# The state-space layer's small products sent to the two halves of the array in turn

## The chip, the cores and the metric

The kernel runs on one core of one Trainium2 chip. A time is the device time of one execution, in microseconds (us). Three timed runs of the kernel before took 2817.99, 2818.27 and 2820.51 us; the median is 2818.27.

## The reference, cut to what matters

One hybrid decoder block on 528 tokens (16 learned ones and 512 of the sequence) of width 2048, all in float32: attention and a state-space layer run side by side on the same normalised input, are mixed by gates, projected, and followed by a dense feed-forward layer. The part that the change touches is the state-space layer, 64 groups of 16 channels, each with 64 complex states:

```python
def s5_scan(u, lam_re, lam_im, log_step, b_re, b_im, c_re, c_im, d):
    ...
    bu_re = jnp.einsum('blgp,gnp->blgn', uf, bb_re)
    bu_im = jnp.einsum('blgp,gnp->blgn', uf, bb_im)
    ...
    _, _, x_re, x_im = lax.associative_scan(combine, (a_re, a_im, bu_re, bu_im), axis=1)
    y = (jnp.einsum('blgn,gpn->blgp', x_re, c_re.astype(f32))
         - jnp.einsum('blgn,gpn->blgp', x_im, c_im.astype(f32))
         + d.astype(f32) * uf)
    return y
```

## The kernel before, in words

The weights stream from HBM in blocks of 128 x 1024. ScalarE rounds each block to a high part `whi` (L261), VectorE subtracts to get the low part `wlo` (L262), and every product of the dense layers is three matmuls (high by high, high by low, low by high). `Weights.use()` splits two blocks ahead of the one in use; three buffers hold raw blocks, three the split ones. TensorE works through the dense layers block by block (`dense()`, L369: eight k-tiles of three matmuls of 512 columns per block).

The state-space layer is a background program: the generator `ssm()` (L508). After each dense block `bg()` (L354) lets it emit work until it has yielded more than the 3.6 us of credit that the block gives; the numbers behind `yield` are prices written by hand. So its instructions stand between dense blocks in TensorE's one queue, in an order that is fixed when the program is built.

The time axis is cut into 66 chunks of 8 steps, and the 64 groups into four batches of 16 (8 pairs `j` with two members `g2` each). In a batch TensorE does four things:

- Kernel taps, `pk` (L667 to L670): for each pair the taps of lags 0 to 7, 128 rows (lag and channel) by 32 columns. The weights `BL` are 128 columns wide; the real and the imaginary part are two products that add up. 16 products. VectorE adds the direct term, and eight DMAs write the taps to HBM (`kd`), from where eight other DMAs build the triangular `TT`.
- Transposes of `BL` (L679), eight of 128 x 128, which ScalarE copies out of PSUM (L680).
- Chunk sums, `pS` (L710 to L717): 32 products of 64 weight columns and 66 moving columns in two bursts. The two members `g2` of a pair write partitions 0 to 63 and 64 to 127 in turn, and each product is a sum by itself.
- Outputs, `pys` (L748 to L753): 64 products of 64 weight columns and 64 moving columns. Each output half `r` of each group is the sum of two, one of `TT` with the inputs `U` and one of `C2` with the states `X2`. `pys[0]` is the PSUM tile V, `pys[1]` the tile Q. All products of the first half (partitions 0 to 63) come first, then, behind a `yield`, all of the second.

In the trace the helper `mm` is L315, so these products are told apart by their tiles: `psQ<-sC,ssA` is `pk`, `psD<-U,ssB` is `pS`, `<-U,ssB` into psV or psQ is the `TT` product (`TT` lies in the buffer ssB) and `<-w,ER` the `C2` product (`X2` lies in w, `C2` in ER). The trace has two records, a weight load (LDWEIGHTS) and a matmul each, for one of these float32 products: the 16 products of `pk` are 32 records.

The code names in full:

Of the kernel before, what the change touches and what calls it, by code (L numbers as in the profile page):

```python
# [30 lines left out]
P = 128  # L31
# [17 lines left out]
BP = 8  # L49
# [236 lines left out]
def build(tc, A, out):  # L286
    nc = tc.nc
    ctx = ExitStack()
    with ctx:
        sp = ctx.enter_context(tc.tile_pool(name="sp", bufs=1))  # L290
        pp = ctx.enter_context(tc.tile_pool(name="pp", bufs=1, space=bass.MemoryType.PSUM))
        dp = ctx.enter_context(tc.tile_pool(name="dp", bufs=1, space=bass.MemoryType.DRAM))
        ctx.enter_context(tc.manual_schedule())
        _emit(nc, sp, pp, dp, A, out)


def _emit(nc, sp, pp, dp, A, out):
# [3 lines left out]
    def sb(shape, dt, tag, bufs=1):  # L301
        cnt[0] += 1
        return sp.tile(shape, dt, tag=tag, name=f"{tag}_{cnt[0]}", bufs=bufs)
# [3 lines left out]
    def ps(shape, tag):  # L307
        cnt[0] += 1
        return pp.tile(shape, F32, tag=tag, name=f"ps{tag}_{cnt[0]}", bufs=BANKS[tag])
# [4 lines left out]
    def mm(o, l, r, start, stop, more=False):  # L314
        PE.matmul(o, lhsT=l, rhs=r, start=start, stop=stop, skip_group_check=more)  # L315
# [5 lines left out]
    def tt(o, a, b, op, eng=DVE):  # L321
        eng.tensor_tensor(o, a, b, op=op)  # L322
# [148 lines left out]
    def halves(tag0, tag1):  # L471
        return [(ps([P, 512], tag0)[:, :HT], 0, HT), (ps([P, 512], tag1)[:, :HT], HT, T)]

    pend = []
    for j in range(8):
        if j == 2:
            d2 = ps([P, 2, 512], "D")
            o = [(d2[:, 0, :HT], 0, HT), (d2[:, 1, :HT], HT, T)]
        else:
            o = halves("A", "B")  # L480
# [24 lines left out]

    MAGIC = 12582912.0

    def ssm():  # L508
        prm = sb([P, 3, 32], F32, "sprm")
        POOL.dma_start(prm, A["sprm"])  # L510
# [99 lines left out]
        for b in range(4):  # L610
# [6 lines left out]
            Ct = sb([P, 2, BP, 48], F32, "sC")  # L617
# [26 lines left out]
            BL = sb([P, 2, BP, CL * 16], F32, "ssA")  # L644
# [20 lines left out]

            pk = ps([P, 512], "Q")
            for j in range(BP):  # L667
                o = pk[:, j * 32:(j + 1) * 32]
                mm(o, BL[:, 0, j], Ct[:, 0, j, 16:48], True, False)
                mm(o, BL[:, 1, j], Ct[:, 1, j, 16:48], False, True)  # L670
            tt(Dg, pk[:, :BG * 16], Dg, ADD)
            for i in range(CL):
                POOL.dma_start(kd[:, g0:g0 + BG, i], Dg[i * 16:(i + 1) * 16].rearrange("p (g o) -> p g o", o=16))
# [36 lines left out]
            for h in range(2):  # L710
                pS = ps([P, 2, 512], "D")
                for jl in range(4):
                    j = h * 4 + jl
# [31 lines left out]
            yield 3.4  # L745
            Y = sb([P, BG, 64], F32, "T1")
            pys = [ps([P, BP, 64], "V"), ps([P, BP, 64], "Q")]
            for r in (slice(0, 64), slice(64, P)):  # L748
                for j in range(BP):
                    for g2 in range(2):  # L750
                        mm(pys[g2][r, j], TT[:, 2 * j + g2, r], U[:, 2 * j + g2, 2:66], True, False)
                        mm(pys[g2][r, j], C2[:, g2, j, r], X2[:, g2, j, 1:65], False, True)
                yield 0.1  # L753
            for g2 in range(2):
                ACT.activation(Y[:, g2::2], pys[g2], AF.Copy)
            yield 3.4
# [5 lines left out]

    left = {"kr", "kv", "q"}
    bg_gen[0] = ssm()
    kvl = sb([P, 4, T], F32, "ssA")
    acc_kv = sb([P, T], F32, "acc")
    for j in range(4):
        o = halves("A", "B")
# [8 lines left out]
    o = halves("A", "B")  # L777
# [801 lines left out]
    def down(fs, ot, c, w):  # L1579
        p = ps([P, 512], "AB"[ot % 2])  # L1580
        o = p[:, :c.stop - c.start]
        for n_, f in enumerate(fs):
            wh, wl = w(ot * len(fs) + n_)
            x = acts[f][:, :, c]
            mm(o, wh, x[:, 0], n_ == 0, False)
            mm(o, wh, x[:, 1], False, False)
            mm(o, wl, x[:, 0], False, n_ == len(fs) - 1)
        return o
# [30 lines left out]
    for h, c in ((0, lo_), (1, hi_)):  # L1619
        for ot in range(KT):  # L1620
            o = down(LAST, ot, c, resident)
# [31 lines left out]
```

## Time and profile before

| | |
|---|---|
| median of the three runs | 2818.27 us |
| the profiled execution | 2820.02 us |
| its span, first to last instruction | 2818.2 us |
| TensorE matmuls busy | 2776.5 us, 99% of the span |
| TensorE weight loads busy | 2562.7 us, 91% |
| VectorE / ScalarE / GpSimd busy | 1908.8 / 1135.9 / 413.8 us |
| mean granted TensorE clock | 0.996 of full |

How to read the rows below. A row of a timeline begins with its start and its length in us, then engine, line, operation, output<-inputs, shapes and a count: "x32" are 32 records that follow each other, and the length runs from the first start to the last end. A number in square brackets is the idle time of that engine ahead of the row and what ended it. PE is the matmul side of TensorE, PEld its weight loads. Matmul records overlap (the next starts while the last is still draining), so what a product costs is read from start to start, not from the length of a record. A row of the view by stretches has the stretch, its length, the busy time and the count of records on each engine, then the granted clock, the share of DMA time and GB/s.

### The profile page before, as it was taken

What the parts mean: (1) busy time and instruction counts of PE and PEld (TensorE: products, weight loads), DVE (VectorE), ACT (ScalarE), POOL (GpSimd) and SP (SyncE); (2) the same over time, 40 slices, a digit from 0 to 9 for tenths busy, and PEclk for the clock granted to TensorE, in tenths of its full rate; (3) what the DMA queues carried; (4) which work ended last, traced back from release to release, by engine and by line L of the source; (5) the groups of instructions that cost most, each with busy time, mean ns of one, the idle gap of its engine ahead of it and who ended that gap; (6) DMA issues with size and microseconds to landing.
All of it is one profiled execution on the core that took longest, in us unless ns stands there. A gap on an engine that the chain in (4) does not pass through costs nothing.

```text
span 2818.2 us, 47282 instructions
## 1 busy us (share of the span) xinstructions
PE 2776.5 (99%) x19526; PEld 2562.7 (91%) x19526; DVE 1908.8 (68%) x2609; ACT 1135.9 (40%) x1625; POOL 413.8 (15%) x633
## 2 busy tenths in 40 slices
PE   9999999999999999999999999999999999999997
PEld 8988888889999788888889999999999998999997
DVE  6467456556666433343468888888888888788896
ACT  5123222225555432222234444444444445353445
POOL 2012221222111000111212000000000003030112
PEclk9999999999999999999999999999999999999999
DMA  5333443542222243334433343333333337474542
GB/s 192 106 117 115 128 142 112 139 132 88 63 68 72 94 142 110 122 116 139 134 128 137 133 150 127 128 135 135 137 129 139 128 128 258 161 261 173 199 161 98
DMA packets 114631, 378.86 MB, mean 134 GB/s; under 512 B 16720, under 2 KB 21584, under 8 KB 114352
## 3 DMA queue, kind: packets, MB, share of 16 engines
q1 hardware_dynamic: 76672, 263.36, 27.5%
q0 software_dynamic: 36320, 109.29, 12.3%
q10 hardware_dynamic: 1424, 3.21, 0.5%
q8 instruction: 153, 2.51, 0.4%
q14 instruction: 62, 0.51, 0.1%
HBM read 316.04 MB, written 51.97 MB: 131 GB/s over the span
## 4 chain that ended last, share of the span: by engine, by line
PE 92%; DVE 3%; DMA 2%; issue 1%; ACT 1%; POOL 0%; DVEq 0%; ACTq 0%; POOLq 0%
PE psA L315 60%; PE psB L315 19%; PE psQ L315 6%; PE psV L315 5%; PE psD L315 2%; DVE S L322 1%; DVE wlo L262 1%; DMA S<-td 0%; DVE ev L322 0%; ACT whi L261 0%; DMA ER<-td 0%; PE psA L1024 0%; DMA T<-td 0%; DMA ssB<-td 0%; DMA raw<-in_wst 0%
## 5 line engine op out<-in xcount | busy, mean ns | idle before, releaser
L315 PE MATMUL psA<-S,whi 128*128 128x256 f32 (+2 forms) x5440 | 1306.6, 327 | 16.9 <-ACT whi L261 6.3
L315 PEld LDWEIGHTS psA<-S,whi 128*128 128x128 f32 x5440 | 921.4, 188 | 115.7 <-ACT whi L261 7.7
L315 PE MATMUL psA<-S,wlo 128*128 128x256 f32 (+2 forms) x2720 | 889.8, 327 | 0.0
L262 DVE TENSOR_TENSOR wlo<-raw,whi 128x1024 fp32r<-128x1024 f32 (+1 forms) x479 | 592.3, 1238 | 310.3 <-ACT whi L261 308.1
L261 ACT ACTIVATE whi<-raw 128x1024 fp32r<-128x1024 f32 (+1 forms) x479 | 504.1, 1054 | 534.7 <-PE psA L315 254.6
L315 PEld LDWEIGHTS psA<-S,wlo 128*128 128x128 f32 x2720 | 513.2, 189 | 47.3
L315 PE MATMUL psB<-S,whi 128*128 128x256 f32 (+1 forms) x1392 | 285.0, 283 | 0.1
L262 DVE TENSOR_TENSOR wlo<-cmb,whi 128x1024 fp32r<-128x1024 f32 x180 | 219.9, 1221 | 67.6 <-ACT whi L261 66.6
L261 ACT ACTIVATE whi<-cmb 128x1024 fp32r<-128x1024 f32 x180 | 190.4, 1058 | 171.3 <-DVE wlo L262 125.0
L315 PEld LDWEIGHTS psB<-S,whi 128*128 128x128 f32 x1392 | 227.1, 189 | 0.3 <-PE psD L315 0.3
L315 PE MATMUL psB<-S,wlo 128*128 128x256 f32 (+1 forms) x696 | 195.9, 281 | 1.5 <-DVE wlo L262 1.5
L315 PEld LDWEIGHTS psB<-S,wlo 128*128 128x128 f32 x696 | 131.6, 189 | 1.7 <-DVE wlo L262 1.7
L1312 POOL DMA_DIRECT2D td<-sC x22 | 15.8, 718 | 754.9 <-ACT ev L1384 712.0
L322 DVE TENSOR_TENSOR H<-psA,ev 128x512 f32<-128x512 f32 x32 | 22.1, 690 | 85.2 <-PE psA L315 85.2
L836 ACT ACTIVATE ev<-ev 128x512 f32<-128x512 f32 x32 | 20.2, 632 | 146.8 <-DVE ev L322 146.8
L242 DVE TENSOR_TENSOR cmb<-raw,raw 128x1024 f32<-128x1024 f32 x60 | 73.1, 1219 | 8.8 <-DMA raw<-in_wst 8.7
L322 POOL TENSOR_TENSOR acc<-acc,ev 128x512 f32<-128x512 f32 (+2 forms) x43 | 53.4, 1241 | 162.0 <-ACT ev L1615 80.6
L315 PE MATMUL psA<-H,whi 128*128 128x264 f32 (+2 forms) x312 | 76.5, 334 | 0.6 <-DVE ev L322 0.5
L242 DVE TENSOR_TENSOR cmb<-cmb,raw 128x1024 f32<-128x1024 f32 x60 | 73.2, 1220 | 0.0
L242 DVE TENSOR_TENSOR raw<-raw,raw 128x1024 f32<-128x1024 f32 x60 | 73.1, 1218 | 0.0
L242 DVE TENSOR_TENSOR cmb<-raw,cmb 128x1024 f32<-128x1024 f32 x60 | 73.1, 1218 | 0.0
L315 PE MATMUL psB<-ssA,whi 128*128 128x256 f32 (+1 forms) x340 | 72.5, 303 | 0.0
(630 smaller groups left out, 4982.9 us busy)
## 6 DMA issues: line engine op xcount, KB each, us to landing
raw<-in_wst SPq DMA_DIRECT2D x485, 512.0 KB, 3.6
td<-sC POOLq DMA_DIRECT2D x22, 512.0 KB, 3.2
td<-H POOLq DMA_DIRECT2D x40, 256.0 KB, 3.3
S<-td POOLq DMA_DIRECT2D x40, 256.0 KB, 8.0
sg<-ev POOLq DMA_DIRECT2D x32, 256.0 KB, 2.3
ev<-sg POOLq DMA_DIRECT2D x32, 256.0 KB, 3.0
U<-ER POOLq DMA_DIRECT2D x64, 64.0 KB, 2.0
ev<-in_xT POOLq DMA_DIRECT2D x16, 256.0 KB, 3.0
```

The source lines that it names most:

```text
L242: self.nc.vector.tensor_tensor(t, g(a), g(b), op=op)
L261: self.nc.scalar.activation(hi[:, a:b], w[:, a:b], AF.Copy)
L262: self.nc.vector.tensor_tensor(lo[:, a:b], w[:, a:b], hi[:, a:b], op=ALU.subtract)
L315: PE.matmul(o, lhsT=l, rhs=r, start=start, stop=stop, skip_group_check=more)
L322: eng.tensor_tensor(o, a, b, op=op)
L836: ACT.activation(e, e, AF.Sigmoid)
L1312: POOL.dma_start(td[pr, 0:2].rearrange("f p n -> p f n"), Cu)
```

## The change

`pk` is cut into output halves: each of its 16 products of 128 weight columns becomes two of 64, one per half of the PSUM partitions, so 32 products. The products of `pys` stay 64, but the loop over the halves moves inward: each `TT` product of the first half is followed by that of the second, then the two `C2` products. The two chunks of `pys` are now cut by pairs (four and four) and not by halves; there are as many yields at the same prices.

```diff
+    RH = slice(0, 64), slice(64, P)
...
             for j in range(BP):
-                o = pk[:, j * 32:(j + 1) * 32]
-                mm(o, BL[:, 0, j], Ct[:, 0, j, 16:48], True, False)
-                mm(o, BL[:, 1, j], Ct[:, 1, j, 16:48], False, True)
+                for i in range(2):
+                    for r in RH:
+                        mm(pk[r, j * 32:(j + 1) * 32], BL[:, i, j, r], Ct[:, i, j, 16:48], i == 0, i == 1)
...
-            for r in (slice(0, 64), slice(64, P)):
-                for j in range(BP):
-                    for g2 in range(2):
+            for j in range(BP):
+                for g2 in range(2):
+                    for r in RH:
                         mm(pys[g2][r, j], TT[:, 2 * j + g2, r], U[:, 2 * j + g2, 2:66], True, False)
+                    for r in RH:
                         mm(pys[g2][r, j], C2[:, g2, j, r], X2[:, g2, j, 1:65], False, True)
-                yield 0.1
+                if j % 4 == 3:
+                    yield 0.1
```

Only TensorE's instructions differ. VectorE, ScalarE, GpSimd and SyncE have the same instructions in the same order in both kernels, and the dense blocks on TensorE stand where they stood.

TensorE at the taps of the first batch, before (psA is the dense block, psB the transposes; the size is that of the output, partitions by columns):

```order
L315 MATMUL psA_2095<-S_31_168,whi_2058 128x512 x2
L315 MATMUL psA_2095<-S_31_168,wlo_2059 128x512
L315 MATMUL psQ_2156<-sC_1933,ssA_2054 128x32 x16
L679 MATMUL psB_2183<-ident_101,ssA_2054 128x128 x4
L679 MATMUL psB_2189<-ident_101,ssA_2054 128x128 x4
```

and after:

```order
L315 MATMUL psA_2095<-S_31_168,whi_2058 128x512 x2
L315 MATMUL psA_2095<-S_31_168,wlo_2059 128x512
L315 MATMUL psQ_2156<-sC_1933,ssA_2054 64x32 x32
L681 MATMUL psB_2199<-ident_101,ssA_2054 128x128 x4
L681 MATMUL psB_2205<-ident_101,ssA_2054 128x128 x4
```

The 16 products with 128 output partitions are 32 with 64 now; nothing around them has moved.

TensorE at the start of the outputs of the first batch, before, with the semaphores that an instruction waits for (DMASW and DMAHW are DMA queues):

```order
L315 MATMUL psV_2786<-U_1937,ssB_2663 64x64 [waits DMASW4_49,DMASW3_49,DMASW5_49,DMASW2_49,Pool_49]
L315 MATMUL psV_2786<-w_2658,ER_2780 64x64 [waits DMAHW4_49,DMAHW1_49,Activation_49]
L315 MATMUL psQ_2787<-U_1937,ssB_2663 64x64
L315 MATMUL psQ_2787<-w_2658,ER_2780 64x64 [waits DMAHW5_49,DMAHW2_49,Activation_49]
L315 MATMUL psV_2786<-U_1937,ssB_2663 64x64
L315 MATMUL psV_2786<-w_2658,ER_2780 64x64
L315 MATMUL psQ_2787<-U_1937,ssB_2663 64x64
```

and after:

```order
L315 MATMUL psV_2802<-U_1937,ssB_2679 64x64 [waits DMASW4_49,DMASW3_49,DMASW5_49,DMASW2_49,Pool_49]
L315 MATMUL psV_2802<-U_1937,ssB_2679 64x64 [waits DMASW6_49,DMASW7_49,DMASW1_49,DMASW0_49]
L315 MATMUL psV_2802<-w_2674,ER_2796 64x64 [waits DMAHW4_49,DMAHW1_49,Activation_49]
L315 MATMUL psV_2802<-w_2674,ER_2796 64x64
L315 MATMUL psQ_2803<-U_1937,ssB_2679 64x64 x2
L315 MATMUL psQ_2803<-w_2674,ER_2796 64x64 [waits DMAHW5_49,DMAHW2_49,Activation_49]
L315 MATMUL psQ_2803<-w_2674,ER_2796 64x64
```

Equal tiles come in pairs now, one product per half. The waits for the DMAs of `TT` that the second half needs (the second row) stood half of all products later before, at the first product of the second half.

## Rows read from the trace of the kernel before

**Rows 1.** The page: the span, and TensorE's two sides.

```profile
span 2818.2 us, 47282 instructions
PE 2776.5 (99%) x19526; PEld 2562.7 (91%) x19526; DVE 1908.8 (68%) x2609; ACT 1135.9 (40%) x1625; POOL 413.8 (15%) x633
```

**Rows 2.** View by stretches: the stage of the state-space layer.

```profile
207.00:620.00 413.00, 410.46 (x2457) 340.07 (x2456) 241.47 (x402) 111.10 (x140) 94.80 (x168) 1.00 0.45 128
```

**Rows 3.** Waits of TensorE, 195 to 660 us: in total, times, longest.

```profile
PE psQ L315 <- ACT whi L261: 1.3, 1, 1.3
PE psB L679 <- ACT ssB L680: 1.1, 4, 0.3
PE psB L315 <- ACT S L1000: 1.1, 1, 1.1
PE psA L315 <- DVE ev L322: 0.5, 1, 0.5
```

**Rows 4.** View by stretches: chunk sums, half of the outputs, all outputs, taps.

```profile
247.52:248.60 1.08, 1.08 (x33) 1.01 (x32) 0.43 (x1) 0.61 (x1) 0.00 (x0) 1.00 0.75 182
300.17:304.04 3.87, 3.87 (x65) 3.80 (x64) 0.69 (x1) 0.12 (x1) 0.00 (x0) 1.00 0.01 4
401.20:408.62 7.42, 7.42 (x129) 7.36 (x128) 0.69 (x1) 0.12 (x1) 0.00 (x0) 1.00 0.01 4
337.43:340.92 3.49, 3.49 (x34) 3.49 (x32) 0.00 (x0) 0.00 (x0) 0.00 (x0) 1.00 0.56 178
```

**Rows 5.** Timeline of TensorE around a burst of chunk sums.

```profile
247.19 0.40 PE L315 MATMUL psA<-S,wlo 128*128 128x512 f32 x1
247.52 1.15 PE L315 MATMUL psD<-U,ssB 128*64 128x66 f32 x32
248.60 0.72 PE L315 MATMUL psA<-S,whi 128*128 128x512 f32 x2
```

**Rows 6.** Instructions by tile: the chunk sums (ns least, median, most).

```profile
L315 PE MATMUL psD<-U,ssB x256: 222/222/273, 247.5 to 578.0; 128*64 128x66 f32 x128
```

**Rows 7.** Timeline of TensorE around the taps of the second batch.

```profile
337.19 0.39 PE L315 MATMUL psA<-S,wlo 128*128 128x512 f32 x1
337.43 3.65 PE L315 MATMUL psQ<-sC,ssA 128*128 128x32 f32 x32
```

**Rows 8.** Timeline of TensorE: the outputs pass from the first to the second half.

```profile
615.22 0.22 PE L315 MATMUL psQ<-U,ssB 128*64 128x64 f32 x1
615.22 0.27 PE L315 MATMUL psV<-U,ssB 128*64 128x64 f32 x1
615.27 0.22 PE L315 MATMUL psQ<-U,ssB 128*64 128x64 f32 x1
```

**Rows 9.** Timeline, the first batch's outputs: TensorE's wait, and the DMA issue before.

```profile
286.41 0.62 ACTq L503 DMA_DIRECT2D ER<-ssA  x1
...
289.29 0.28 PE L315 MATMUL psQ<-U,ssB 128*64 128x64 f32 x2
290.92 0.30 PE L315 MATMUL psQ<-w,ER 128*64 128x64 f32 x2 [1.35 <-ACT whi L261]
...
294.41 0.74 PE L315 MATMUL psA<-S,whi 128*128 128x512 f32 x2
```

**Rows 10.** DMA issues by line, 255 to 300 us: KB each, us to landing.

```profile
ER<-ssA ACTq DMA_DIRECT2D x2, 256.0 KB, 3.8
```

**Rows 11.** Timeline of ScalarE and VectorE behind the last batch's outputs.

```profile
618.97 0.60 ACT L755 ACTIVATE T<-psV 128x512 f32<-128x512 f32 x1 [9.72 <-PE psV L315]
...
620.46 1.06 ACT L261 ACTIVATE whi<-raw 128x1024 fp32r<-128x1024 f32 x1
...
621.55 1.23 DVE L262 TENSOR_TENSOR wlo<-raw,whi 128x1024 fp32r<-128x1024 f32 x1 [9.09 <-ACT whi L261]
```

## The prediction, as it was put on record before the changed kernel ran

> **What bounds the kernel now.** I read the page first: TensorE's matmuls are busy for 2776.5 of 2818.2 us, its weight loads for 91% of them [rows 1]. An average over all stages can mislead, so the second view is the stage that holds all edited products: between 207 and 620 us TensorE is busy for 410.46 of 413.00 us, at a granted clock of 1.00, while VectorE has work for 241.47 us and ScalarE for 111.10 us [rows 2]. The third is what TensorE waits for there: four kinds, 4.0 us in all [rows 3]. So in this stage the end is set by how fast TensorE gets through its queue, and time taken out of that queue is worth itself, as long as no producer falls behind. Last come the starts of single products, since the lengths of records overlap and say little on cost. All the change does is to reorder and cut products in this queue; the other engines' orders are the same.
>
> **What a product costs on one half, and what in two halves.** The kernel before already has a burst that sends products to the two halves in turn: the chunk sums. 32 records (16 products of 64 weight columns and 66 moving columns) go from 247.52 to 248.60 us, 1.08 us, to the next dense matmul [rows 4]. The burst's row is 1.15 us long up to the end of its last record [rows 5], a record lasts 222 ns [rows 6], so the last record starts at 247.52 + 1.15 - 0.22 = 248.45. That is 0.93 us for 31 steps: 30 ns from record to record. Behind the last start there are 0.15 us until the dense matmul at 248.60 [rows 5]. Ahead of the burst there are 0.33 us from the last dense start (247.19), where the taps, which use the whole width as the dense products do, need 0.24 us (337.19 to 337.43) [rows 5, 7]; so going over to half width costs 0.09 us.
>
> The outputs, today all on one half and then all on the other, take 3.87 us for 64 records [rows 4]. Less 0.15 us at the end, 63 steps cost 3.72 us: 59 ns each, twice the 30 ns of the chunk sums, with the same weight columns and two moving columns less. The trace even shows the outputs doing what the change asks of them, once per batch: where the first half ends and the second begins, a record into psQ (first half) and one into psV (second half) both start at 615.22 [rows 8]. The taps take 3.49 us for 32 records of 128 weight columns, 109 ns each [rows 4].
>
> I take 30 ns for every record of the changed products: it comes from the nearest row there is, with the same weight width. The low end is 29 ns (30 scaled by 64/66) with nothing at the end, worth 1 to 2 us more in all; the high end is 59 ns, halves that don't run beside each other at all.
>
> **The outputs, step by step.**
> - Batches two to four: 128 records in one go, 7.42 us before [rows 4]. After: 127 x 0.030 + 0.15 = 3.96. Gain 3.46 each, 10.38 for three.
> - First batch, second burst: 64 records, 3.87 before, 63 x 0.030 + 0.15 = 2.04 after. Gain 1.83.
> - First batch, first burst: here TensorE waits. The first product of `C2` into psQ starts at 290.92 after 1.35 us of idle time [rows 9]. The row names ScalarE, but that instruction waits for two DMA queues as well, and the copy of `C2` issued at 286.41 [rows 9] lands 3.8 us later by the median of its kind [rows 10], which fits better. The wait stays: in the new order TensorE gets there with 12 records behind it and not 6, in about the same time (12 x 30 against 6 x 59 ns). Behind it 52 records are left: 51 x 0.030 + 0.15 = 1.68 us, where 290.92 to 294.41 was 3.49 [rows 9]. Gain 1.81.
>
> Together 14.02 us. The second half's share of `TT` is awaited at the second product now and not in the second half of the work. I cost that at nothing: TensorE's waits in this stage [rows 3] have no row for `TT`, whose eight DMAs are issued on one queue in one run, and the first half needs the last four of these already; if that cover were gone it would cost the landing of a DMA, 4 us for the first batch alone.
>
> **The taps.** 32 records of 128 columns become 64 of 64. Entering half width costs 0.09, 63 steps cost 1.89, leaving costs 0.15: 2.13 us against 3.49. Gain 1.36, four times: 5.44 us. Here the nearest row is a little further off, since the moving side is 32 columns and not 66; the step then hangs on the weight loads alone. From below: were 64-column loads half of a 128-column one (54 ns) and strictly one after the other, 64 of them would take 3.5 us, and with entry and exit 0.24 us per batch would be lost. The chunk sums speak for 30: their 32 loads lie in 1.01 us [rows 4], so loads of 64 columns into different halves can't take 54 ns one after the other.
>
> **What is late next.** Behind the outputs ScalarE, which had waited 9.72 us for them, copies them out, then splits the next block of weights at 620.46; VectorE ends that block's low part at 621.55 + 1.23 = 622.78 [rows 11]. This block is used two blocks later, a block takes 5.76 us (294.41 to the burst at 300.17) [rows 4, 9], so there are some 8 us to spare; and the whole chain starts at TensorE's last output product, so it moves forward with it. The waits of [rows 3] for the transposes' copies are counted from the taps' end, and stay.
>
> Sum: 14.02 + 5.44 = 19.46 us. The profiled execution took 2820.02 us, 1.8 around its span of 2818.2; it would become 2800.6. The median of the runs lies 1.75 us below the profiled one: 2818.27 - 19.46 = 2798.8, and I say 2799.
>
> **Rivals.**
> - *The halves don't run side by side for these products* (the change doesn't do what it says). Both halves stream the same columns of `U` at the same moment, where the two products of a pair of chunk sums stream different ones, and each output is a sum of two products, where a chunk sum stands alone. Then the outputs stay at 59 ns and gain nothing, the taps lose 4 x 0.24: 2819. [...] Both halves here use all 128 rows. [...] Against it stands this trace: the chunk sums' halves share all rows too, and their 32 loads and matmuls take 1.08 us [rows 4], and the outputs overlap at 615.22 [rows 8]. Chance 0.05.
> - *The taps alone fail*: with 32 moving columns the loads become the limit, as bounded above. 14.02 - 0.96 = 13.1 gained: 2805. Chance 0.07.
> - *Half of the gain is given back* at a producer that was just in time, such as the copy of `C2` of the first batch [rows 9] in the other batches. Against it: in those the outputs run 7.42 us without a gap [rows 4]. 2818.27 - 9.7 = 2809. Chance 0.06.
> - *Slower: each change of half drains the array.* Leaving half width cost 0.15 us where a step is 0.03, so a drain may be worth 0.12 us. If a product that adds to an earlier one has to see the array drained when the half changes, the taps pay it 31 times and the outputs 63 times per batch: 94 x 0.12 = 11.3 us against a gain of 4.8, four times +6.5: 2844. It decides from 4.82 / 94 = 51 ns per change. The chunk sums change halves 15 times within 0.93 us [rows 5], and the two records of each product add up too; that leaves little room. Chance 0.02.
>
> **How the numbers follow.** The forecast has 0.80, with its own range of 2795 to 2803 (both ends of the 30 ns above, entry and exit, and 1 to 2 us between runs). The range reaches over the failed taps to 2808 and leaves out part of the half gain, the nil gain and the slower case. A measurement of this kernel can tell 0.2%, 5.6 us, from no change: faster is below 2812.6. The forecast, the failed taps and nearly all of the half gain lie there, 0.92; the nil gain and a rest make 0.06 within; 0.02 slower.
>
> **What would show it.** In the profile after, the stretch of outputs of a later batch should be about 4.0 us from its first product to the next dense matmul, and the taps about 2.0 us to the first transpose; the dense matmuls around should keep their distances, and TensorE's waits in this stage should stay near 4 us. The span's loss should be the sum of these eight or nine stretches. Output stretches of 7.4 us would prove the first rival, taps of 3.7 the second, new rows of TensorE's waits on `psQ<-w,ER` or on the dense blocks the third, stretches above 7.5 us the fourth.

## The result, and the profile after

The changed kernel takes 2796.65 us (median of four runs, 2795.21 to 2798.50) against 2819.39 us for the kernel before in the same rounds: a ratio of 0.9918, 95% interval 0.9905 to 0.9930, that is 22.7 us less (20 to 27). The forecast was 2799, the range 2794 to 2808.

The page of the changed kernel, answering to [rows 1]:

```profile
span 2796.7 us, 47538 instructions
PE 2753.9 (98%) x19654; PEld 2537.8 (91%) x19654; DVE 1908.9 (68%) x2609; ACT 1136.4 (41%) x1625; POOL 414.5 (15%) x633
```

TensorE has 128 records more (4 x 32 for the taps), its busy time falls by 22.6 us and the span by 21.5; the other engines' busy time stays. The view by stretches of the changed kernel, in the order of [rows 4], then the stage as in [rows 2]:

```profile
246.52:247.60 1.08, 1.08 (x33) 1.01 (x33) 0.38 (x2) 0.63 (x1) 0.00 (x0) 1.00 0.66 163
297.37:299.38 2.01, 2.01 (x65) 1.95 (x64) 0.69 (x1) 0.11 (x1) 0.00 (x0) 1.00 0.00 0
395.28:399.16 3.88, 3.88 (x129) 3.81 (x128) 0.69 (x1) 0.12 (x1) 0.00 (x0) 1.00 0.02 7
332.87:334.86 1.99, 1.99 (x65) 1.95 (x64) 0.00 (x0) 0.00 (x0) 0.00 (x0) 1.00 0.84 235
207.00:600.00 393.00, 390.57 (x2592) 318.79 (x2591) 241.37 (x402) 112.04 (x141) 94.83 (x168) 1.00 0.48 135
```

The chunk sums, untouched, are at 1.08 us again. The outputs fall from 3.87 to 2.01 and from 7.42 to 3.88 us; the taps do twice the records in 1.99 us, not 3.49. Less 0.15 us at the end, that is 29.4 ns a record for the outputs and 29.2 for the taps.

What TensorE waits for in this stage, against [rows 3]:

```profile
PE psQ L315 <- ACT whi L261: 1.3, 1, 1.3
PE psB L681 <- ACT ssB L682: 1.1, 4, 0.3
PE psB L315 <- ACT S L1004: 1.1, 1, 1.1
PE psA L315 <- DVE ev L322: 0.5, 1, 0.5
```

Not one new wait, and none longer. Timeline of TensorE at the first batch's outputs, against [rows 9]:

```profile
287.88 0.34 PE L315 MATMUL psV<-U,ssB 128*64 128x64 f32 x4
...
289.96 0.34 PE L315 MATMUL psQ<-w,ER 128*64 128x64 f32 x4 [1.32 <-ACT whi L261]
...
291.63 0.74 PE L315 MATMUL psA<-S,whi 128*128 128x512 f32 x2
```

The wait for the copy of `C2` stays (1.32 for 1.35 us), and from its end to the dense block it is 1.67 us, where before had 3.49. ScalarE behind the last batch's outputs, against [rows 11]:

```profile
598.11 0.60 ACT L759 ACTIVATE T<-psV 128x512 f32<-128x512 f32 x1 [6.04 <-PE psV L315]
...
599.60 1.06 ACT L261 ACTIVATE whi<-raw 128x1024 fp32r<-128x1024 f32 x1
```

It waits 6.04 us for them, not 9.72; the split of the next weights follows 1.5 us behind the outputs, as before.

**The sum.** Outputs: 3 x 3.54 + 1.86 + 1.82 = 14.30 us. Taps: 3.49 - 1.99, less 0.09 for going over to half width, is 1.41, four times 5.64. Together 19.94, but the span fell by 21.5. Nearly all of the rest lies at one place, the third batch's taps. Timeline of the kernel before there:

```profile
441.87 3.69 PE L315 MATMUL psQ<-sC,ssA 128*128 128x32 f32 x32
445.37 1.10 PE L679 MATMUL psB<-ident,ssA 128*128 128x128 f32 x4
446.12 1.20 PE L315 MATMUL psA<-S,whi 128*128 128x512 f32 x2
...
452.94 1.04 PE L679 MATMUL psB<-ident,ssA 128*128 128x128 f32 x8
```

and of the changed kernel:

```profile
432.50 2.06 PE L315 MATMUL psQ<-sC,ssA 128*64 128x32 f32 x64
434.49 0.66 PE L681 MATMUL psB<-ident,ssA 128*128 128x128 f32 x4
434.90 0.71 PE L315 MATMUL psA<-S,whi 128*128 128x512 f32 x2
...
440.53 1.03 PE L681 MATMUL psB<-ident,ssA 128*128 128x128 f32 x8
```

From the taps to the second group of transposes it was 11.07 us and is 8.03: 3.04 less, of which the taps are 1.51. The first dense pair took 1.20 us, now 0.71. The view by stretches of the kernel before tells why (the number before the last two is the granted clock):

```profile
440.00:444.00 4.00, 4.00 (x29) 3.64 (x28) 0.00 (x0) 0.00 (x0) 0.00 (x0) 1.00 0.76 254
444.00:448.00 4.00, 4.00 (x23) 3.61 (x23) 1.02 (x2) 1.45 (x3) 1.69 (x3) 0.67 0.05 4
448.00:452.00 4.00, 4.00 (x17) 3.26 (x16) 3.15 (x15) 0.61 (x1) 3.81 (x10) 0.91 0.56 97
```

The granted clock was 0.67 from 444 to 448 us and 0.91 from 448 to 452 us, though TensorE was never idle: 4.00 of 4.00 us busy. In the changed kernel it is 1.00 in each stretch of 4 us from 428 to 444 us, and the 1.53 us are gone: 19.94 + 1.53 = 21.47. The stage itself bears this out: from the last dense start ahead of the first taps (207.25 us before, 207.80 after) to the first dense start behind the last outputs (619.10 and 598.22) it is 21.43 us shorter. That the whole span lost the same 21.5 us is in part luck. The stage begins 0.55 us later after the change; behind it the profile of before has two more falls of the clock, at 923 us (granted 0.90 from 920 to 924 us, 0.67 from 924 to 928) and at 1497 us (0.58 from 1496 to 1500 us, 0.99 from 1500 to 1504), which the profile after doesn't have there; an estimate of their cost, the busy time of these stretches (2.46, 3.34, 3.18 and 4.00 us) times what the clock lacked, is 2.7 us; and small losses elsewhere make up for both.

### The profile page after: what moved, and what is told of

Read it like the earlier page. It is cut to its first block, busy times and chain, and to the rows that moved or that the text cites. A ratio compares the mean times of both kernels' runs of the same rounds, so it can differ in the third digit from the quotient of the medians.

```text
span 2796.7 us, 47538 instructions
## 1 busy us (share of the span) xinstructions
PE 2753.9 (98%) x19654; PEld 2537.8 (91%) x19654; DVE 1908.9 (68%) x2609; ACT 1136.4 (41%) x1625; POOL 414.5 (15%) x633
## 4 chain that ended last, share of the span: by engine, by line
PE 91%; DVE 3%; DMA 2%; issue 2%; ACT 1%; POOL 0%; DVEq 0%; ACTq 0%; POOLq 0%
PE psA L315 60%; PE psB L315 19%; PE psQ L315 5%; PE psV L315 4%; PE psD L315 1%; DVE wlo L262 1%; DVE S L322 1%; DMA S<-td 0%; DMA raw<-in_wst 0%; DVE ev L322 0%; PE psA L1028 0%; ACT whi L261 0%; DMA T<-td 0%; DMA ssB<-td 0%; DMA H<-td 0%
```

## The experiments

Two questions were left: when the halves run side by side, and whether the clock belongs to the change. Times without a ratio are single runs; the kernel before took 2821.10 us (median of eleven) beside the half-by-half taps and the runs of two, and 2818.50 or 2818.58 us (one run each) beside the others.

**Outputs alone.** The taps as before:

```diff
-                for i in range(2):
-                    for r in RH:
-                        mm(pk[r, j * 32:(j + 1) * 32], BL[:, i, j, r], Ct[:, i, j, 16:48], i == 0, i == 1)
+                o = pk[:, j * 32:(j + 1) * 32]
+                mm(o, BL[:, 0, j], Ct[:, 0, j, 16:48], True, False)
+                mm(o, BL[:, 1, j], Ct[:, 1, j, 16:48], False, True)
```

> Only the outputs go to the two halves in turn; the taps are the 16 full-width products of before. If the gain is made of the two stretches and nothing else, the outputs take 3.88 us (before 7.42) in batches two to four and 2.01 and 3.75 us in the first, the taps stay at 3.49 us, and the kernel takes 14.4 us less than before: 2805.0 us, ratio 0.9949. The rival: part of the gain is TensorE's clock, which in the profile of before is granted at 0.67 from 444 to 448 us, right behind full-width taps. Then such a fall may show here again behind one of the four tap stretches, and this kernel gains 2 to 3 us less than the whole change lacks by the taps alone.

Measured: 2806.18 us, ratio 0.9944 (0.9931 to 0.9958). By stretches, the outputs, the taps, and two places behind taps:

```profile
398.46:402.34 3.88, 3.88 (x129) 3.81 (x128) 0.69 (x1) 0.12 (x1) 0.00 (x0) 1.00 0.05 19
435.74:439.22 3.48, 3.48 (x33) 3.48 (x32) 0.00 (x0) 0.00 (x0) 0.00 (x0) 1.00 0.31 117
212.00:216.00 4.00, 4.00 (x19) 3.30 (x18) 3.50 (x22) 2.11 (x4) 4.00 (x8) 0.69 0.33 27
440.00:444.00 4.00, 4.00 (x12) 3.10 (x11) 2.32 (x7) 2.06 (x3) 3.86 (x7) 0.61 0.28 23
```

The outputs' gain is there in full, and the granted clock falls behind two of the four taps (0.69 and 0.61).

**Taps alone.** The outputs' two loops in the order of before.

> Only the taps go to the two halves in turn; the outputs are first all of one half, then all of the other, as before. By the stretches: taps 1.99 us plus 0.09 for going over to half width, where before had 3.49, so 1.41 us four times, 5.6 us: 2813.8 us, ratio 0.9980. The outputs stay at 7.42 us. If the fall of the clock behind the taps belongs to the full-width taps, the gain is 1.5 to 2.5 us more, 2811.5 to 2812.5 us, and no stretch between 200 and 620 us has a granted clock below 0.99.

Measured: 2813.64 us, ratio 0.9974 (0.9964 to 0.9985), 7.3 us less (4 to 10). The stretches of outputs and taps:

```profile
398.88:406.31 7.43, 7.43 (x130) 7.36 (x129) 0.69 (x1) 0.13 (x1) 0.00 (x0) 1.00 0.02 4
439.80:441.79 1.99, 1.99 (x66) 1.95 (x65) 0.00 (x0) 0.00 (x0) 0.00 (x0) 1.00 0.54 189
```

No stretch between 200 and 620 us has a granted clock below 1.00. The gain is nearer to taps with clock (7.1 to 8.1) than to taps without (5.6), but the interval holds both. The two parts add up: 0.56% + 0.26% against 0.82%.

**Taps half by half.** `for r in RH` outermost.

> The taps are cut into halves, but all products of the first half come ahead of all of the second; the outputs as in the change. If the pace within one half is set by the load of 64 weight columns, a step is 59 ns as it was for the outputs of before: 62 steps and the exit are 3.8 us where the change has 1.99. The rival: the pace within a half is set by the moving columns, 32 here where the outputs have 64; then a step is some 30 ns with no change of half, and the stretch stays near 2.0 us.

Measured: 2802.83 us. A tap stretch:

```profile
435.39:439.04 3.65, 3.65 (x66) 3.60 (x65) 0.00 (x0) 0.00 (x0) 0.00 (x0) 1.00 0.35 125
```

(3.65 - 0.15) / 63 = 55.5 ns with 32 moving columns, where the outputs of before had 59 ns with 64, and the taps of before 109 ns with 128 weight columns and 32 moving ones. So the step is near 59 ns with the same 64 weight columns and half the moving ones, and about half of 109 ns with half the weight columns and the same moving ones: within one half it goes with the weight columns here. When the halves alternate, the 64 weight loads of the taps, 138 ns each by the median of their records, lie in 1.95 us (332.87 to 334.82), and a record costs 29.2 ns.

**Longer runs on one half.** The change goes to the other half after each product, two records. Three kernels do it after two, four and eight products; the first by

```diff
                     for r in RH:
                         mm(pys[g2][r, j], TT[:, 2 * j + g2, r], U[:, 2 * j + g2, 2:66], True, False)
-                    for r in RH:
                         mm(pys[g2][r, j], C2[:, g2, j, r], X2[:, g2, j, 1:65], False, True)
```

and the others with the loops over `g2` and over two pairs inside that over `r`.

> The outputs change half after every two products (four records) and not after each one. One theory: matmuls start in the order of the queue, and only the first record of a run starts together with the last record of the run before it, on the other half; then a run of n records costs n-1 steps of 59 ns. For n = 2, the change, that is 29.5 ns a record; for n = 4 it is 44 ns, 32 runs of 3 steps and the exit: 5.8 us per batch, where the change has 3.88. The rival: TensorE looks far ahead and works through the two halves independently; then 128 records still take 3.9 us. A third: a product that adds to the one ahead of it waits for it; then more than 5.8 us.

> The outputs change half after every four products, eight records. Runs of two products cost 3.93 us per batch, so the theory that only one record of a run overlaps with the run before has fallen; TensorE looks further ahead. How far shows in the outputs of before: at their one change of half 128 records took 7.42 us where twice 63 steps of 59 ns, one more step and the exit are 7.64, so some 3 to 4 records overlapped there. If that is the reach, a run of eight costs about 4.5 steps of 59 ns: 16 x 4.5 x 0.059 + 0.15 = 4.4 us per batch. If the reach is a whole run of eight and more, the stretch stays at 3.9 to 4.0 us.

> The outputs change half after every eight products, 16 records. With a reach of 3 to 4 records a run costs 12 to 13 steps of 59 ns: 8 x 12.5 x 0.059 + 0.15 = 6.0 us per batch. With a reach of 16 records or more, 3.9 to 4.1 us. In between, the stretch tells the reach: each record of reach takes 8 x 0.059 = 0.47 us off 7.7 us.

Measured: 2798.85, 2804.32 and 2807.46 us. The outputs of the second batch, by stretches, after two products:

```profile
395.35:399.28 3.93, 3.93 (x130) 3.86 (x129) 0.69 (x1) 0.13 (x1) 0.00 (x0) 1.00 0.03 6
```

after four, with two stretches of the first batch's outputs, where the clock fell too, behind the wait for `C2`:

```profile
397.83:402.75 4.92, 4.92 (x130) 4.85 (x129) 0.69 (x1) 0.13 (x1) 0.00 (x0) 1.00 0.05 18
288.00:292.00 4.00, 2.52 (x35) 2.38 (x35) 1.23 (x1) 1.39 (x2) 0.00 (x0) 0.77 0.77 230
292.00:296.00 4.00, 4.00 (x42) 3.59 (x39) 0.00 (x0) 0.00 (x0) 0.00 (x0) 0.80 0.32 117
```

and after eight:

```profile
397.45:403.80 6.35, 6.35 (x129) 6.28 (x128) 0.69 (x1) 0.12 (x1) 0.00 (x0) 1.00 0.02 8
```

My first theory (only one record overlaps at each change) wanted 5.8 us for runs of two products and fell: 3.93. Taken as steps of 59 ns, 4.92 us are 81 steps where 127 would be without overlap, so 15 changes save 46, 3.1 each; 6.35 us are 105 steps, 7 changes save 22, 3.1 each; the kernel before, with one change, 123 steps, 3.8. So an estimate from these times is that about three records of a run start beside the first ones of the next run. The timeline of the first batch in runs of four products, at a granted clock of 0.77, shows as much: the next run's first record starts into psV at 290.57 us, and three of the run before start behind it, into psQ at 290.67, 290.77 and 290.88. The forecasts of 4.4 and 6.0 us had reckoned with 3 to 4 and were too low. Of the 3.54 us that the change gains per batch, runs of four records lose next to nothing (0.05), runs of eight 1.04 and runs of 16 2.47.

**Quarters.** Four slices of 32 partitions in place of the two of 64, in one kernel for the outputs and in another for the taps:

```diff
+    RQ = [slice(32 * i, 32 * i + 32) for i in range(4)]
...
-                    for r in RH:
+                    for r in RQ:
```

> The outputs go to four quarters (32 partitions) in turn, so 256 records per batch of 32 weight columns and 64 moving columns. Runs of four and of eight products gave a reach of about three records (4.92 and 6.36 us). If the queue's reach of three records is what limits, at most four records are under way, two quarters' worth: the pace stays near 29 ns a record and the outputs take 7.5 us, 3.6 us more per batch than in the change. If the quarters work independently, a record costs half of 29 ns and the stretch stays at 3.9 us.

> The taps go to four quarters in turn, 128 records of 32 weight columns and 32 moving columns, where the change has 64 of 64 columns in 1.99 us. In one half taps cost 55 ns a record, set by the load of 64 columns; a load of 32 columns should cost half, 28 ns. With a reach of three records two quarters overlap: 14 ns a record and the stretch stays at 2.0 us. If a record can't be issued faster than about 29 ns, the pace of the change, the stretch is 127 x 0.029 + 0.15 = 3.8 us.

Measured: 2801.10 and 2792.70 us. The outputs in quarters, third and second batch, by stretches:

```profile
495.36:499.08 3.72, 3.72 (x258) 3.63 (x257) 0.69 (x1) 0.09 (x1) 0.00 (x0) 1.00 0.43 135
394.69:399.71 5.02, 3.92 (x257) 3.70 (x256) 0.69 (x1) 0.10 (x1) 0.00 (x0) 1.00 0.07 23
```

256 records in 3.72 us are 14 ns each, half of 29, which is what the second theory forecast. But there are twice as many records, so the outputs gain next to nothing (3.72 for 3.88 us). And in two of three batches TensorE stands still once, for something that the profile does not name, so that they take 5.02 and 5.11 us; from the timeline of the second batch:

```profile
398.34 0.32 PE L315 MATMUL psV<-w,ER 128*32 128x64 f32 x8 [1.10 <-issue]
```

What coincides with it is on the DMA side. The DMA queue that the page calls `q8 instruction` moved 153, 154 and 158 packets in the kernel before, the change and this one, which have 39052, 39308 and 40332 records of TensorE: one packet for 255 of them in each. Both standstills end 2.3 us after such a packet starts (396.02 to 398.34 us, 597.20 to 599.54 us); in the batch without one, no packet starts from the first record until 498.64 us, when the burst is nearly over. That instructions came late is an estimate from these times; no run tried it.

The taps in quarters, by stretches:

```profile
430.57:431.79 1.22, 1.22 (x129) 1.18 (x128) 0.00 (x0) 0.00 (x0) 0.00 (x0) 1.00 0.82 292
```

Both theories were wrong here: the 128 records start within 1.10 us (430.57 to 431.67), 1.10 / 127 = 8.7 ns each, no floor near 29 ns, and more overlap than two quarters would give (14 ns). Counted per quarter, that is 35 ns a record with 32 moving columns, where the outputs have 4 x 14 = 56 ns with 64 moving columns and the same 32 weight columns. So in quarters the slower of the two is the one with more moving columns, which may be why the outputs gain next to nothing there; no run changed the moving side alone. The expected 2.0 us came from a reach of three records over the whole queue, and 1.22 us are less than that. About three records for each part of the array by itself would fit; that is an estimate from these times (4.92, 6.35, 3.72 and 1.22 us), and nothing in the trace shows it.

**The clock: full-width taps twice, half-width taps twice, and before once more.**

```diff
+            for j in [*range(BP)] * 2:
+                o = pk[:, j * 32:(j + 1) * 32]
+                mm(o, BL[:, 0, j], Ct[:, 0, j, 16:48], True, False)
+                mm(o, BL[:, 1, j], Ct[:, 1, j, 16:48], False, True)
```

> The full-width taps of before, all of them computed twice over (the second time over the first), the outputs as in the change. The tap stretches take 6.98 us. If the falls of the granted clock behind the taps (in one of four batches of the kernel before and in two of four with the outputs alone changed, in none of twelve with half-width taps) belong to full-width taps, they come more often now: behind or within at least three of the four stretches, each costing up to 2 us beside the 3.5 us that the second taps cost. If they came by chance, there are none or one.

> The control to the full-width taps twice: half-width taps, twice over, all of the first half ahead of all of the second, so that the stretch is about as long (128 records of 55 to 58 ns, 7.2 us) and has as few columns. If what lets the clock fall is full width, no stretch between 200 and 620 us has a granted clock below 0.99. If it is a long stretch of short products of whatever width, the clock falls here as often as there.

> The kernel before once more, for a second profile of its clock: with full-width taps the granted clock should fall behind some of the four tap stretches, one or two, as it did at 444 us; if that fall was a matter of chance, none. The stretches themselves as in the first profile: taps 3.49, outputs 7.42 us.

Measured: 2835.23, 2818.95 and 2820.04 us. The four tap stretches at full width twice over:

```profile
207.60:217.17 9.57, 9.57 (x65) 9.57 (x64) 0.00 (x0) 0.00 (x0) 0.00 (x0) 0.73 0.17 53
341.69:352.14 10.45, 10.45 (x65) 10.45 (x64) 1.81 (x2) 0.37 (x1) 0.00 (x0) 0.66 0.36 122
450.74:461.03 10.29, 10.29 (x65) 10.29 (x64) 0.00 (x0) 0.00 (x0) 0.00 (x0) 0.67 0.12 47
565.66:574.93 9.27, 9.27 (x66) 9.27 (x64) 0.00 (x0) 0.00 (x0) 0.00 (x0) 0.75 0.09 34
```

and at half width twice over, half by half:

```profile
209.32:216.70 7.38, 7.38 (x129) 7.34 (x129) 0.00 (x0) 0.00 (x0) 0.00 (x0) 1.00 0.24 72
339.33:346.71 7.38, 7.38 (x129) 7.34 (x129) 1.29 (x2) 0.00 (x0) 0.00 (x0) 1.00 0.46 145
444.35:451.73 7.38, 7.38 (x130) 7.34 (x129) 0.00 (x0) 0.00 (x0) 0.00 (x0) 1.00 0.15 61
554.78:562.16 7.38, 7.38 (x130) 7.34 (x129) 0.00 (x0) 0.00 (x0) 0.00 (x0) 1.00 0.12 45
```

and, from within the first stretch at full width, 4 us with TensorE busy all the time and a granted clock of 0.50:

```profile
212.00:216.00 4.00, 4.00 (x21) 4.00 (x20) 0.00 (x0) 0.00 (x0) 0.00 (x0) 0.50 0.00 0
```

At full width the granted clock is 0.66 to 0.75 in all four stretches, which take 9.27 to 10.45 us for 6.98: 2.3 to 3.5 us each within the stretches alone, more than the 2 us that I had put as the most. At half width, in stretches of 7.38 us and with the same products, it is 1.00 in all four. The two kernels also differ in the records of a stretch (64 and 128), so the runs don't separate width from the rate of records. The second profile of the kernel before has two falls, behind the first and the third taps:

```profile
212.00:216.00 4.00, 4.00 (x18) 3.26 (x17) 3.52 (x23) 1.94 (x4) 4.00 (x8) 0.65 0.34 27
...
448.00:452.00 4.00, 4.00 (x14) 3.22 (x13) 2.69 (x12) 1.14 (x2) 4.00 (x8) 0.71 0.48 49
```

Over all profiles: full-width taps once over, a fall behind 5 of 12 stretches (1, 2 and 2 of 4 in the three kernels that have them); taps in halves or quarters once over, 0 of 36 (nine profiles). Behind the stage the clock falls too, far from any taps: granted 0.66 from 2376 to 2380 us before, 0.65 from 2356 to 2360 us after the change; no run here explains these falls.

**The taps in quarters, timed.** The same kernel as above, run more than once.

> The taps in quarters again, the outputs in halves as in the change, timed in five rounds. One profile of it shows taps of 1.22 us where the change has 1.99, four times: 3.1 us less than the change's 2796.65, 2793.6 us, a ratio to the kernel before of 0.991 or a little less. If that profile was only a good run, the time is that of the change, 2796 to 2797 us.

Measured: 2794.05 us, the median of 2793.25, 2793.34, 2794.76 and 2801.98, ratio to the kernel before 0.9901 (0.9884 to 0.9917). The change has 0.9918 (0.9905 to 0.9930), so by ratio it is 0.17% less; the two were timed in different rounds, and their intervals overlap. By the stretches, which take 0.77 us less four times, it should be 3.1 us better than the change; the times alone don't show it. The run of 2801.98 us is the profiled one: its taps take 1.23 us, as short as in the first profile, and it loses about 8 us against that profile behind 2340 us, outside the stage.

## Why the prediction was right

- *TensorE's queue sets the end of this stage, so time out of it counts in full.* Right: waits the same row by row, and the stage is 21.43 us shorter, of which the edited stretches and the clock explain all (21.47).
- *30 ns a record, from the chunk sums.* Right: 29.4 and 29.2. The outputs gained 14.30 us for 14.02, the taps 5.64 for 5.44. The low end of the bound, 29, was the nearer one.
- *0.09 us to go over to half width, 0.15 to leave it.* Right: the taps start 0.32 us behind the last dense start (332.55 to 332.87), and each stretch comes within 0.08 us of its forecast.
- *The rival that halves don't run side by side*: wrong here. Both halves, and all four quarters, use all 128 rows, and 128 records in turn take 3.88 us where one half after the other took 7.42, 256 records in quarters 3.72. What the rival feared, the same `U` columns streamed twice at once and sums of two products, costs nothing that shows.
- *The taps alone fail, since the loads are the limit.* The step within one half is near what this rival reckoned with (55.5 ns for 54), but it doesn't follow that the taps gain nothing: with the halves in turn 64 loads lie in 1.95 us, where 64 steps of 54 ns would be 3.5.
- *Half of the gain given back, or a drain at each change of half.* Neither has a row. Runs of one product and of two take 3.88 and 3.93 us, so going to the other half twice as often costs nothing measurable.
- *What was not in the sum*: the clock. I read 1.00 for the whole stage from one row of 413 us [rows 2] and for the second batch's taps [rows 4] and looked no closer; a fall to 0.67 and 0.91 in the two stretches of 4 us at one tap stretch does not show in such a mean. It is worth 1.5 us in the profile of before and makes, with 0.5 us from the pace, the difference between the forecast 19.5 us and the 21.47 found in the stage. So the sign that the span's loss is the sum of the edited stretches did not hold (19.94 of 21.5). The medians differ by 22.7 us; what lies between that and 21.5 is within the scatter of the runs and has no row.

## What to carry to other kernels

Where products with few weight columns stand in a row, write them so that neighbours go to different column parts of the array: with parts of 64 the pace doubled here (59 to 29.4 ns a record for the outputs, 55.5 to 29.2 for the taps), as long as a part got no more than four records before the other had its turn. Parts of 32 took another 0.77 us off each tap stretch, with 32 moving columns, but next to nothing off the outputs, with 64. For the wide product with few moving columns here the cut paid: the full-width taps cost 109 ns a record for 32 moving columns, two halves 2 x 29.2 = 58.4 ns. Look for a burst in the same trace that already has the wished pattern: it gave the gain of the edited stretches to 3% (19.46 for 19.94 us).

## What the hardware showed that was not expected

- In the doubled stretches of full-width taps, with 32 moving columns, the granted clock of TensorE fell while TensorE was busy all the time: 0.50 from 212 to 216 us, within the first stretch, and 0.66 to 0.75 in the mean of each of the four; in bursts of 7.38 us at half width it was 1.00. Why is open; the runs only show width, and with it the rate of records, on one side and the clock on the other.
- The taps' records, sent to four quarters in turn, started 8.7 ns after one another in the mean, over 127 steps (1.10 us).
- Bursts of 256 records that need under 4 us met a standstill of 1.10 and 1.18 us in two of three batches. Both ended 2.3 us after a packet of `q8 instruction` had started; that this is the cause was not tried.
